# 48 unused columns instead of 16 between two groups of weight buffers in an encoder kernel

## The chip, the core and the metric

The kernel runs on one core of one Trainium2 chip, as one launch. The metric is the device time of that launch in microseconds (us); less is better. Before the change, three runs took 2910.47, 2912.47 and 2912.86 us: the median is 2912.47 us.

## What is computed

The reference is a two-layer bidirectional encoder on 256 tokens of width 2048, in float32. Nearly all of its arithmetic is in products of the 256 tokens with weight matrices:

```python
for i in range(DEPTH):                          # 2 layers
    h = rmsnorm(x, g_mix[i])
    z = h @ w_in[i]                             # q, k, v, two latents, rope key, two gates
    ...                                         # two kinds of attention: y_diff, y_mla
    merged = jax.nn.sigmoid(ga) * y_diff + jax.nn.sigmoid(gb) * y_mla
    x = x + merged @ w_out[i]
    gu = rmsnorm(x, g_ffn[i]) @ w_gate_up[i]    # 2048 -> 2 x 5632
    gate, up = jnp.split(gu, 2, axis=-1)
    x = x + (jax.nn.silu(gate) * up) @ w_down[i]
    e = p[i] @ w_ple_in[i]
    x = x + jax.nn.sigmoid(rmsnorm(x, g_ple[i]) @ w_ple_gate[i]) * e
return rmsnorm(x, g_final)
```

## The kernel before, in words

**A product in three parts.** Tokens lie along the columns, features along the 128 partitions. Each float32 number is cut in two numbers of the type fp32r: its leading bits ("hi") and the remainder ("lo"). A product of weights W and activations u is then W_hi·u_hi + W_hi·u_lo + W_lo·u_hi. An activation tile `ua[j]` or `ub[j]` (the operands) holds 256 columns of u_hi and behind them 256 columns of u_lo for one block of 128 features, so 512 columns or 2048 bytes in each partition.

For one block of 128 × 128 weights, `emit` issues two matmuls. The first (line 211) has 128 columns of `whi` as stationary operand and streams all 512 columns of the tile past them; the second (line 212) has 128 columns of `wlo` and streams the first 256 columns, u_hi. I call the two a pair. The profile shows each matmul as a weight load (PEld, LDWEIGHTS) and the matmul proper (PE, MATMUL). `product` runs 16 pairs into one PSUM bank for an output block of 128 features (8 to 16 for the other widths). Here are the lines:

```python
PE.matmul(acc, hi[:, s], u, start=start, stop=False)          # line 211: weights hi, 512 columns
PE.matmul(acc[:, T:], lo[:, s], u[:, :T], start=False, stop=stop)  # line 212: weights lo, 256 columns
```

**The weights' way.** `piece` fetches 1024 columns of float32 weights by one DMA from SyncE's queue into one of four buffers `w32`; ScalarE copies them to fp32r, which is `whi` (line 181, three buffers); VectorE subtracts, which gives `wlo` (line 74 through a helper, three buffers). One such piece serves 8 pairs.

**The values' product** (`values`, lines 392 to 394) is the other way round: slices of `ua` are stationary, and 512 columns of `whi` (lines 392 and 393) or `wlo` (line 394) stream past them. Attention's scores are line 341, its transposes 359, its outputs 563 and 620.

**What sets the order.** A scheduler at build time puts each engine's instructions in a fixed order, and the engines meet through semaphores. The stages follow the reference: values, latents, queries and keys between attention heads; the two gates (`wga`, `wgb`); the branch products (`w_bd`, `w_bm`); `w_out`; the feed-forward products; `w_pg`.

**Where the buffers lie.** Buffers are laid out one behind the other in each partition, in the order in which they are first asked for. Start addresses, modulo 256 bytes, before the change:

| buffers | bytes each | address modulo 256 |
|---|---|---|
| `ua`, `ub` (all 32) | 2048 | 128 |
| `xT`, `kr`, `fb`, `fc`, `fa5` to `fa7`, cosines and sines | 1024 and more | 128 |
| `ident`, `ones`, `fa0` to `fa4` | 512, 2048 | 32 |
| `w32` (4), `wlo` (3) | 4096 | 128 |
| `step` | 64 | 128 |
| `whi` (3) | 4096 | 192 |
| `E`, `join`, `a`, `sq`, `sh`, `E1`, `wt`, `sig`, `vals` | 1024 and more | 192 |
| `row`, `ssq`, `dg` | 1024 | 64 |

A slice of 128 columns is 512 bytes, so every slice of a buffer has that buffer's place modulo 256. Nothing reads `step`: it is set to zero once, by GpSimd, and keeps 16 columns (64 bytes) between `wlo` and what follows. It is made in `piece`, between `lo` and `hi`:

```python
if not step:
    step.append(wts.tile([P, STEP], F32, tag="step", name="step", bufs=1))
    nc.gpsimd.memset(step[0], 0.0)
hi = wts.tile([P, PT * P], F32R, tag="whi", name="whi", bufs=3)
```

Of the kernel before, what the change touches and what calls it, by code (L numbers as in the profile page):

```python
# [37 lines left out]
W_BUFS = 4  # L38
WARM = 8
PAD = 96  # L40
STEP = 16
NO_SYNC = mybir.DependencyInfo(mybir.DependencyClass.NoSync, mybir.DependencyReason.DATA)

TWO_PI = 2.0 * math.pi
# [8 lines left out]
def encoder(ctx, tc, x, p, positions, cols, lams, wq, wk, wv, wcq, wckv, wkr, wga, wgb,  # L53
# [114 lines left out]
    def piece(src, n):  # L168
# [3 lines left out]
# [3 lines that stand above are left out]
# [614 lines left out]
```

## Time and profile before

| what | value |
|---|---|
| median of three runs | 2912.47 us |
| the profiled execution's own time | 2910.11 us |
| its span, from the first instruction to the last | 2908.3 us |
| mean granted TensorE clock | 0.998 |
| TensorE busy with matmuls | 2890.7 us |
| VectorE, ScalarE busy | 2062.3 us, 1524.6 us |
| HBM read | 527.43 MB |

The profile comes from one execution. A row of a group names the line, the engine, the operation, what is written from what, the number of instructions, then the busy time, the mean duration of one in ns, and the idle time of the engine ahead of them. Matmuls are pipelined: the recorded duration of one reaches from its start to its modelled end and overlaps the next one's, so what one matmul costs is read from start to start.

### The profile page before, as it was taken

To read this page: it belongs to the slowest core of one execution; us is meant where nothing else is said; L and a number is where in the kernel's file an instruction comes from. 1 tells how busy PE (TensorE), PEld (TensorE's weight loads), DVE (VectorE), ACT (ScalarE), POOL (GpSimd) and SP (SyncE) were. 2 spreads that over 40 slices of the span, in tenths; PEclk is the share of its full clock that TensorE was granted. 3 is DMA by queue.
4 is the path that set the end of the run, shared out by engine and by line. 5 is a ranking of instruction groups with operands and counts; after the bars stand their busy time and mean duration, and the time that the engine had idled before them with its cause. 6 is when DMAs were issued, how large, how long until landed. Compare 5 with 4: busy or idle time off the path is not lost.

```text
span 2908.3 us, 43980 instructions
## 1 busy us (share of the span) xinstructions
PE 2890.7 (99%) x16750; PEld 2539.6 (87%) x16750; DVE 2062.3 (71%) x3529; ACT 1524.6 (52%) x2529; POOL 1.7 (0%) x9
## 2 busy tenths in 40 slices
PE   9999999999999999999999999999999999999998
PEld 7888888888888888888888888888888888888887
DVE  7897658776666666667859976687666666666676
ACT  6676545554444444454646755555444444444554
POOL 0000000000000000000000000000000000000000
PEclk9999999999999999999999999999999999999999
DMA  7554466555665566566565445666556655655664
GB/s 236 165 163 147 159 195 197 190 186 188 184 193 189 183 189 192 189 188 188 189 188 168 151 153 167 195 195 189 186 188 184 193 188 180 197 188 189 189 186 141
DMA packets 156019, 532.40 MB, mean 183 GB/s; under 512 B 16928, under 2 KB 23840, under 8 KB 155808
## 3 DMA queue, kind: packets, MB, share of 16 engines
q1 hardware_dynamic: 155376, 529.01, 57.9%
q8 instruction: 131, 2.15, 0.3%
q14 instruction: 80, 0.66, 0.1%
q10 hardware_dynamic: 432, 0.59, 0.1%
HBM read 527.43 MB, written 2.10 MB: 182 GB/s over the span
## 4 chain that ended last, share of the span: by engine, by line
PE 99%; DVE 1%; ACT 0%; DMA 0%; SPq 0%; issue 0%; DVEq 0%
PE mm L211 61%; PE mm L212 31%; PE S L341 1%; PE mmv L394 1%; PE mmv L392 1%; PE mmv L393 1%; PE at L359 0%; PE at L563 0%; PE at L620 0%; DMA w<-in_wv 0%; PE at L280 0%; DVE xT L74 0%; PE at L271 0%; DVE wlo L74 0%; ACT whi L181 0%; DVE a L74 0%
## 5 line engine op out<-in xcount | busy, mean ns | idle before, releaser
L181 ACT ACTIVATE whi<-w 128x1024 fp32r<-128x1024 f32 (+2 forms) x1029 | 1068.5, 1039 | 1311.4 <-issue 749.3
L74 DVE TENSOR_TENSOR wlo<-w,whi 128x1024 fp32r<-128x1024 f32 (+2 forms) x1029 | 1228.6, 1194 | 740.2 <-ACT whi L181 730.4
L211 PE MATMUL mm<-ub,whi 128*128 128x512 f32 x3952 | 1381.5, 394 | 0.0
L211 PE MATMUL mm<-ua,whi 128*128 128x512 f32 x3744 | 1307.8, 394 | 0.0
L212 PE MATMUL mm<-ub,wlo 128*128 128x256 f32 x3952 | 1107.7, 280 | 0.0
L212 PE MATMUL mm<-ua,wlo 128*128 128x256 f32 x3744 | 1048.5, 280 | 0.0
L211 PEld LDWEIGHTS mm<-ub,whi 128*128 128x128 f32 x3952 | 742.1, 188 | 164.5
L211 PEld LDWEIGHTS mm<-ua,whi 128*128 128x128 f32 x3744 | 702.5, 188 | 151.5
L212 PEld LDWEIGHTS mm<-ub,wlo 128*128 128x128 f32 x3952 | 749.0, 190 | 0.8
L212 PEld LDWEIGHTS mm<-ua,wlo 128*128 128x128 f32 x3744 | 708.2, 189 | 2.2 <-DVE wlo L74 0.4
L74 DVE TENSOR_TENSOR a<-mm,join 128x256 f32<-128x256 f32 x421 | 174.8, 416 | 0.3 <-ACT join L236 0.2
L236 ACT ACTIVATE join<-mm 128x256 f32<-128x256 f32 x453 | 165.9, 367 | 5.4 <-PE mm L212 5.0
L74 DVE TENSOR_TENSOR xT<-xT,mm 128x256 f32<-128x256 f32 x256 | 106.6, 419 | 48.4 <-PE mm L212 44.5
L74 DVE TENSOR_TENSOR a<-a,row 128x256 f32<-128x256 f32 x207 | 87.2, 424 | 6.6 <-ACT row L284 0.8
L74 DVE TENSOR_TENSOR a<-a 128x256 f32<-128x256 f32 x120 | 51.0, 425 | 4.0
L392 PE MATMUL mmv<-whi,ua 128*128 128x512 f32 x128 | 51.0, 399 | 2.0 <-ACT whi L181 2.0
L74 DVE TENSOR_TENSOR ua<-a,ua 128x256 fp32r<-128x256 f32 x120 | 50.1, 417 | 1.0 <-ACT ua L244 1.0
L393 PE MATMUL mmv<-whi,ua 128*128 128x512 f32 x128 | 50.5, 395 | 0.0
L244 ACT ACTIVATE ua<-a 128x256 fp32r<-128x256 f32 x120 | 48.2, 402 | 2.7 <-DVE a L74 2.6
L350 ACT ACTIVATE E<-S,nm 128x256 f32<-128x256 f32 x96 | 44.2, 470 | 5.1 <-DVE nm L80 5.0
L394 PE MATMUL mmv<-wlo,ua 128*128 128x512 f32 x128 | 46.8, 397 | 0.1
L74 DVE TENSOR_TENSOR ssq<-ssq,sq 128x256 f32<-128x256 f32 x97 | 40.5, 417 | 0.5 <-ACT sq L263 0.5
(154 smaller groups left out, 1158.9 us busy)
## 6 DMA issues: line engine op xcount, KB each, us to landing
w<-in_w_gate SPq DMA_DIRECT2D x176, 512.0 KB, 4.6
w<-in_w_up SPq DMA_DIRECT2D x176, 512.0 KB, 4.5
w<-in_w_down SPq DMA_DIRECT2D x128, 512.0 KB, 3.7
w<-in_wga SPq DMA_DIRECT2D x64, 512.0 KB, 3.8
w<-in_wgb SPq DMA_DIRECT2D x64, 512.0 KB, 4.5
w<-in_w_out SPq DMA_DIRECT2D x64, 512.0 KB, 4.2
w<-in_w_pg SPq DMA_DIRECT2D x64, 512.0 KB, 4.4
w<-in_w_down SPq DMA_DIRECT2D x64, 384.0 KB, 3.6
```

What stands on the lines that cost most here:

```text
L74: return V.tensor_tensor(out=o, in0=a, in1=b, op=op)
L181: last_split[:] = A.activation(hi[:, :m], w[:, :m], AF.Copy), tt(lo[:, :m], w[:, :m], hi[:, :m].bitcast(F32), ALU.subtract)
L211: PE.matmul(acc, hi[:, s], u, start=start, stop=False)
L212: PE.matmul(acc[:, T:], lo[:, s], u[:, :T], start=False, stop=stop)
L236: A.activation(t, acc[:, T:], AF.Copy)
L244: return A.activation(hi, src, AF.Copy), tt(lo, src, hi.bitcast(F32), ALU.subtract)
L341: PE.matmul(S[:, b, :], q[:, b * P : (b + 1) * P], k, start=j == 0, stop=j == len(pairs) - 1)
L350: last_exp[0] = A.activation(E[:, b, :], S[:, b, :], AF.Exp, bias=nm[:, b : b + 1], scale=scale, accum_out=sm[:, b : b + 1])
L392: PE.matmul(banks[b], xh, hi[:, s], start=a + j == 0, stop=False)
L393: PE.matmul(banks[b], xl, hi[:, s], start=False, stop=False)
L394: last_mm[:] = [PE.matmul(banks[b], xh, lo[:, s], start=False, stop=a + j == n - 1)]
```

## The change

One constant is changed, and with it the size of `step`:

```diff
@@ -38,7 +38,7 @@
 WARM = 8
 PAD = 96
-STEP = 16
+STEP = 48
```

`step` has 192 bytes instead of 64, so everything behind it lies 128 bytes further on: `whi`, and all buffers of the pools for temporary tiles and statistics. `ua`, `ub`, `w32`, `wlo` and all tiles ahead of them stay where they are. Modulo 256, `whi` goes from 192 to 64: from 64 bytes behind the operands' place to 64 bytes ahead of it. `E`, `join`, `a`, `vals`, `wt` and their like go from 192 to 64 too, and `row`, `ssq`, `dg` from 64 to 192. The instructions of every engine and their order are the same, but for the size of one memset on GpSimd.

## The prediction

> **What bounds the kernel now.** I read the page first: busy shares, granted clock, and the chain of work that ended last.
>
> ```profile
> PE 2890.7 (99%) x16750; PEld 2539.6 (87%) x16750; DVE 2062.3 (71%) x3529; ACT 1524.6 (52%) x2529; POOL 1.7 (0%) x9
> ...
> PEclk9999999999999999999999999999999999999999
> ...
> PE 99%; DVE 1%; ACT 0%; DMA 0%; SPq 0%; issue 0%; DVEq 0%
> ```
>
> TensorE is busy in 99% of the span, at full clock in every slice, and the chain runs through it for 99%. Whether it waits for anybody is answered by the waits of PE and PEld; these are the longest rows of each:
>
> ```profile
> PE at L280 <- DVE dg L80: 2.7, 1, 2.7
> PE at L271 <- ACT ssq L260: 2.0, 1, 2.0
> ...
> PEld mmv L392 <- ACT whi L181: 2.8, 2, 1.5
> ```
>
> Waits of 2.7 us in 2908.3 are nothing: the time is the matmuls' own pace, so only a change of pace can show. The page's groups say which matmuls:
>
> ```profile
> L74 DVE TENSOR_TENSOR wlo<-w,whi 128x1024 fp32r<-128x1024 f32 (+2 forms) x1029 | 1228.6, 1194 | 740.2 <-ACT whi L181 730.4
> L211 PE MATMUL mm<-ub,whi 128*128 128x512 f32 x3952 | 1381.5, 394 | 0.0
> L211 PE MATMUL mm<-ua,whi 128*128 128x512 f32 x3744 | 1307.8, 394 | 0.0
> L212 PE MATMUL mm<-ub,wlo 128*128 128x256 f32 x3952 | 1107.7, 280 | 0.0
> L212 PE MATMUL mm<-ua,wlo 128*128 128x256 f32 x3744 | 1048.5, 280 | 0.0
> ```
>
> There are 3952 + 3744 = 7696 pairs. So 1 ns on each pair is 7.7 us, or 0.26% of the time. Durations overlap, so the pace comes from the starts. The timeline in a long feed-forward stretch:
>
> ```profile
> 1101.93 0.39 PE L211 MATMUL mm<-ub,whi 128*128 128x512 f32 x1
> 1101.93 0.19 PEld L212 LDWEIGHTS mm<-ub,wlo 128*128 128x128 f32 x1
> 1102.16 0.28 PE L212 MATMUL mm<-ub,wlo 128*128 128x256 f32 x1
> 1102.16 0.19 PEld L211 LDWEIGHTS mm<-ub,whi 128*128 128x128 f32 x1
> 1102.28 0.40 PE L211 MATMUL mm<-ub,whi 128*128 128x512 f32 x1
> ```
>
> Two things are to be seen. From one line 211 to the next it is 0.35 us: 0.23 for 512 columns and 0.12 for 256. And each weight load starts together with the matmul ahead of its own. So while line 212 streams u_hi (place 128 modulo 256), the next `whi` is loaded (192 before, 64 after); while line 211 streams, `wlo` is loaded (128, as before). The change touches the first of these two overlaps and leaves the second.
>
> Is 0.35 us the pace everywhere? Busy time and count of line 211 in stretches of the span (us, then PE busy with its count; length over count is the pace):
>
> ```profile
> 346.00:529.00 183.00, 182.27 (x537) 100.62 (x536) 1.00 0.62 197
> 529.00:627.00 98.00, 97.41 (x280) 52.34 (x280) 1.00 0.59 188
> 627.00:1450.00 823.00, 822.07 (x2350) 440.94 (x2349) 1.00 0.61 188
> ...
> 1500.00:1550.00 50.00, 48.93 (x144) 26.85 (x143) 1.00 0.58 183
> ...
> 1786.00:1970.00 184.00, 183.27 (x540) 101.17 (x539) 1.00 0.61 197
> 2068.00:2885.00 817.00, 816.07 (x2332) 437.70 (x2332) 1.00 0.60 187
> ```
>
> It is not. 98/280, 823/2350 and 817/2332 are 350 ns a pair; 183/537 and 184/540 are 341, and 50/144 is 347 with its edges in it. From the starts inside these quick stretches:
>
> ```profile
> 399.68 0.39 PE L211 MATMUL mm<-ua,whi 128*128 128x512 f32 x1
> ...
> 400.02 0.39 PE L211 MATMUL mm<-ua,whi 128*128 128x512 f32 x1
> ...
> 401.04 0.39 PE L211 MATMUL mm<-ua,whi 128*128 128x512 f32 x1
> ```
>
> 1.36 us for four pairs: 340 ns. The tiles, the buffers and all their places are the same as in the slow stretches, and other engines' work is much alike. So there are two paces, 340 and 350, that the pair can settle in, and once in one it stays for hundreds of pairs. At equal addresses the phase between load and stream, set by what ran just ahead, decides which. The addresses can only decide which paces exist and how easily each is entered.
>
> **The change, part by part.** The larger memset runs on GpSimd, which is busy for 1.7 us in all, and nobody waits for `step`: nothing. ScalarE writes `whi`, VectorE reads it, and both write and read the shifted temporaries. Should an access cost them something there, the group of `wlo` above bounds what is harmless: one split takes 1.19 us, one piece lasts 8 pairs or 2.8 us, and VectorE idles for 740.2 us ahead of these instructions. Up to some 0.7 us more for each of the 1029 splits is hidden under the matmuls; without that cover each would cost its own excess. I take 0.
>
> On TensorE, line 212's overlap counts. I look for the nearest rows with a load at the stream's place less 64: the values' product. There `whi` (192) streams while a slice of `ua` or `ub` (128) is loaded, in lines 392 and 393: 128 − 192 = −64. In line 394 `wlo` streams (128): difference 0. Each line by itself (duration min/median/max in ns), with scores that have difference 0 behind them:
>
> ```profile
> L392 PE MATMUL mmv<-whi,ua x128: 387/394/793, 4.6 to 1496.0; 128*128 128x512 f32 x128
> L392 PE MATMUL mmv<-whi,ub x16: 391/396/401, 231.1 to 1680.6; 128*128 128x512 f32 x16
> L393 PE MATMUL mmv<-whi,ua x128: 388/393/612, 5.2 to 1496.3; 128*128 128x512 f32 x128
> L393 PE MATMUL mmv<-whi,ub x16: 391/396/398, 231.3 to 1680.8; 128*128 128x512 f32 x16
> L394 PE MATMUL mmv<-wlo,ua x128: 388/393/578, 6.1 to 1496.5; 128*128 128x512 f32 x128
> L394 PE MATMUL mmv<-wlo,ub x16: 389/398/401, 231.5 to 1681.0; 128*128 128x512 f32 x16
> ...
> L341 PE MATMUL S<-kr,fc x48: 279/283/284, 285.4 to 1768.5; 128*128 128x256 f32 x48
> ```
>
> In the same products, difference −64 has medians of 393.5 (the two lines with `ua`) and 396 (with `ub`), difference 0 has 393 and 398. Weighted by 128 and 16, −64 is (128 × 0.5 − 16 × 2)/144 = 0.2 ns dearer than 0. Line 211, also at 0, has 394 as its mean. So −64 looks no different from the places already in use, and all of these rows spread by 5 to 9 ns between minimum and median, as two paces 10 ns apart for two matmuls would make them. The step from −64 against 0 to −64 against +64 is a choice: line 212 at +64 has a mean of 280, and the scores at 0 a median of 283, which lets +64 be up to 3 ns better than 0. I take 0.2 ns on 7696 pairs, 1.5 us, as the likeliest, and keep both ends: below, all pairs at 340; above, 3 ns on each load and the quick stretches lost.
>
> The rest of TensorE: the 2 × 144 matmuls of lines 392 and 393 go from −64 to +64, and the transposes (line 359) read `E` at another distance from `ident`. Even ±3 ns on 288 + 128 of them is 1.2 us. The scores read only tiles that stay. Lines 563 and 620 have both operands among the shifted ones. I take 0.
>
> The sum: 2910.1 us of the profiled execution + 1.5 = 2911.6; the median of the runs shown lies 2.4 us above that execution, so 2914 us.
>
> A rule that bears on this stands in the Trainium skill, "TensorE: Matmul & The Clock Gate", section "Part 2: What happens when you issue a matmul": TensorE has two independent read ports into SBUF, and loading the next weights takes nothing from the running matmul. The same page's "Back-to-back issue gap" has N/2.4 + 2.5 ns, which I work out, as an estimate, to 215.8 + 109.2 = 325 ns for a pair. The trace disagrees with the second, 340 and 350 ns measured, and two paces at one clock are hard to have if streams and loads never meet. By the first rule the sum would be 2912.5 exactly.
>
> **The rivals.**
>
> *Nothing at all (D).* If the two paces come from the order of issue alone and places in SBUF don't matter, every stretch stays as it is: 2912.5 us. For it: equal addresses give both paces. Against it: something has to make 340 into 350, and the median of 283 for scores against 280 for line 212 goes with the place. The Trainium skill's rule on the two ports, above, would give the same.
>
> *The quick pace spreads (B).* At 340 ns in all stretches, the 7696 − 537 − 144 − 540 = 6475 pairs at 350 save 10 ns each: 65 us, to 2848 us. For it: 340 is stable over 500 pairs and differs from 350 only in how it was entered; line 393 reaches the low 388 ns at −64 too. Against: the values' medians at −64 sit with the slow pace. Half of the stretches would give 2880.
>
> *A heavier pace (C).* The load of `whi` at −64 falls on the stream at a worse moment. It shows in line 212, which would go from 280 to 283 or more, and it decides against the change as soon as the quick stretches go: their 537 + 144 + 540 = 1221 pairs at 350 cost 12 us, 2925 us; 3 ns more on every line 212 is another 23, 2948 us; if line 211 is pulled along by 3 ns as well, 2971. For it: 396 in the rows with `ub`, 283 in the scores. Against: 16 instructions each, between other work.
>
> **How the numbers follow.** The forecast (A), two paces much as now with some shift in the quick share, has 0.34: 2906 to 2926 by itself, about half of it within 0.2%. D has 0.10, B 0.30, C 0.26. A difference under 0.2%, 5.8 us, can't be told from none. Faster: 0.30 from B and 0.06 from A. Same: 0.16 from A and 0.10 from D. Slower: 0.26 from C and 0.12 from A. The range goes from B's end, 2848, to C's, 2971; beyond lie a pace under 340, and loads that cost over 3 ns on both matmuls, together under 0.2.
>
> **What would show it.** Right: starts of line 211 still 350 ns apart in the long stretches (about 2350 in 627 to 1450 us) and 340 in 346 to 529 us; mean of line 212 within 1 ns of 280. B: counts near 2420 in 823 us. C: line 212 at 283 or more, no stretch at 340. Wrong in the whole reasoning: TensorE waiting for `whi` or `wlo`, or a pace that differs by stage with no relation to these two.

## The result, and the profile after

The kernel takes 2868.07 us (median of 6 runs, 2865.90 to 2868.81) against 2911.7 us before: a ratio of 0.985, interval 0.9837 to 0.9863. It is faster by 1.5%, a small change but clear of the noise. The profiled execution took 2867.58 us with a span of 2865.8 us, 42.5 us less than that of before. My forecast was no change, 2914 us; the time lies in the stated range, near the side of the rival "the quick pace spreads".

The page after, busy shares and the two matmul groups of the pairs:

```profile
PE 2845.8 (99%) x16750; PEld 2507.7 (88%) x16750; DVE 2063.3 (72%) x3529; ACT 1524.2 (53%) x2529; POOL 1.7 (0%) x9
...
PEclk9999999999999999999999999999999999999999
...
L211 PE MATMUL mm<-ub,whi 128*128 128x512 f32 x3952 | 1360.8, 392 | 0.0
L211 PE MATMUL mm<-ua,whi 128*128 128x512 f32 x3744 | 1283.4, 390 | 0.0
L212 PE MATMUL mm<-ub,wlo 128*128 128x256 f32 x3952 | 1096.8, 278 | 0.0
L212 PE MATMUL mm<-ua,wlo 128*128 128x256 f32 x3744 | 1036.3, 277 | 0.0
```

TensorE is still the bound, at the same clock. Its busy time fell by 44.9 us and the span by 42.5, so the gain is all in the matmuls' pace. Both matmuls of a pair last a little less (line 211 from 394 to 391 ns on average, line 212 from 280 to 277.5), but durations overlap; what a pair costs is read from the starts. Over some 7500 pairs that follow each other directly, a pair takes 342.1 ns on average against 348.1 before. Line 211 (from its start to that of line 212) went from 231.2 to 227.9, line 212 from 116.9 to 114.2. VectorE and ScalarE are as busy as before.

Where? Line 211's count in stretches of the span after (the columns are the stretch, its length, PE busy with the count, PEld busy with its count, clock, DMA share, GB/s):

```profile
346.00:517.00 171.00, 171.00 (x504) 94.38 (x504) 1.00 0.61 195
528.00:604.00 76.00, 76.00 (x224) 41.91 (x224) 1.00 0.60 195
623.00:768.00 145.00, 144.85 (x414) 77.83 (x414) 1.00 0.59 186
840.00:990.00 150.00, 150.00 (x442) 82.80 (x442) 1.00 0.59 192
1100.00:1250.00 150.00, 150.00 (x442) 82.77 (x441) 1.00 0.60 194
1356.00:1427.00 71.00, 71.00 (x203) 38.02 (x203) 1.00 0.60 189
```

150/442 and 171/504 are 339 ns, 145/414 and 71/203 are 350. (A count takes in the matmuls that reach over the edges of its stretch, so length over count reads up to about 1 ns low: by the starts, 1100 to 1250 us is at 350.0 ns before and 340.0 after.) So there are again two paces, 340 and 350, and the quick one now holds nearly everywhere: 5920 of the 7500 pairs take at most 343 ns, against 1546 before. These 4374 pairs at 10 ns each are 44 us. Slow are, apart from a few short pieces, two stretches in each layer, those behind the two norms of the feed-forward and gate parts. The start of the gate part's shows how the pace is lost there, at four small matmuls of the norm (line 271):

```profile
1345.41 0.39 PE L211 MATMUL mm<-ub,whi 128*128 128x512 f32 x1
...
1345.75 0.39 PE L211 MATMUL mm<-ub,whi 128*128 128x512 f32 x1
...
1346.10 0.50 PE L271 MATMUL at<-ones,ssq 128*128 128x1 f32 x4
...
1346.89 0.40 PE L211 MATMUL mm<-ub,whi 128*128 128x512 f32 x1
...
1347.24 0.40 PE L211 MATMUL mm<-ub,whi 128*128 128x512 f32 x1
...
1347.59 0.40 PE L211 MATMUL mm<-ub,whi 128*128 128x512 f32 x1
```

Ahead of them it is 340 ns from start to start, behind them 350. The slow pace isn't quite that of before, either: there line 211's durations alternate, 0.39 and 0.40 us, and the pairs take 348 and 352 ns (or 349 and 351) in turn; here each pair takes 350.

### The profile page after: what moved, and what is told of

The parts are those of the page before. It is cut to its first block, busy times and chain, and to the rows that moved or that the text cites. A ratio compares the mean times of both kernels' runs of the same rounds, so it can differ in the third digit from the quotient of the medians.

```text
span 2865.8 us, 43980 instructions
## 1 busy us (share of the span) xinstructions
PE 2845.8 (99%) x16750; PEld 2507.7 (88%) x16750; DVE 2063.3 (72%) x3529; ACT 1524.2 (53%) x2529; POOL 1.7 (0%) x9
## 4 chain that ended last, share of the span: by engine, by line
PE 98%; DVE 1%; ACT 0%; DMA 0%; issue 0%; SPq 0%; DVEq 0%
PE mm L211 61%; PE mm L212 31%; PE S L341 1%; PE mmv L394 1%; PE mmv L393 1%; PE mmv L392 1%; PE at L359 0%; PE at L563 0%; PE at L620 0%; DMA w<-in_wv 0%; DVE wlo L74 0%; DVE a L74 0%; PE at L280 0%; DVE xT L74 0%; ACT E L350 0%
## 5 line engine op out<-in xcount | busy, mean ns | idle before, releaser
L211 PE MATMUL mm<-ub,whi 128*128 128x512 f32 x3952 | 1360.8, 392 | 0.0
L211 PE MATMUL mm<-ua,whi 128*128 128x512 f32 x3744 | 1283.4, 390 | 0.0
L212 PE MATMUL mm<-ua,wlo 128*128 128x256 f32 x3744 | 1036.3, 277 | 0.0
```

## The experiments

Three theories stood at the start. **Place**: the place of `whi` against the operands decides. **Temporaries**: the tiles that moved along, which stand in the matmuls between stretches, set the phase at which a stretch is entered. **Lots**: any shift draws the entries anew, with no rule.

### Which of the moved buffers does it

`whi` moved alone, or everything else moved alone; a second unused tile behind `whi` does it, and the order of instructions stays that of before.

```diff
 # whi moved alone
-STEP = 16
+STEP = 48
 # both runs
         hi = wts.tile([P, PT * P], F32R, tag="whi", name="whi", bufs=3)
+        if len(step) == 1:
+            step.append(wts.tile([P, 32], F32, tag="behind", name="behind", bufs=1))
+            nc.gpsimd.memset(step[1], 0.0)
```

`whi` alone. Expected:

> whi at the operands' place less 64 as after the change, all temporary tiles back at their places of before (32 unused columns behind whi). If the place of whi against the operands decides (theory 1): 2868 us, within 6 us, and 340 ns a pair in the same long stretches as after. If the moved temporaries, which are stationary or streamed in the matmuls between the stretches, set the phase at which a stretch is entered (theory 2): 2912 us. If any shift draws the entries anew, with no rule (theory 3): any value between 2850 and 2925, as likely near one as near the other.

Measured: 2867.08 us (ratio 0.9851, 0.9835 to 0.9867). The stretches of the matmul with `whi`, same columns:

```profile
346.00:515.00 169.00, 169.00 (x498) 93.30 (x497) 1.00 0.61 195
621.00:759.00 138.00, 137.80 (x394) 73.89 (x393) 1.00 0.59 186
840.00:988.00 148.00, 148.00 (x437) 81.76 (x436) 1.00 0.61 192
1100.00:1249.00 149.00, 149.00 (x439) 82.24 (x439) 1.00 0.61 194
```

The whole gain is there, with the same slow stretch behind the norm (138/394 is 350) between the same quick ones. What the place of `whi` is counted from isn't shown by this: `ua` and `ub` were never moved, and no run moved `whi` by a full 256 bytes. "Against the operands" and "modulo 256" are my way of naming a place.

The temporaries alone. Expected:

> The counterpart: whi at the operands' place plus 64 as before the change, the temporaries 128 bytes further on as after it. Theory 1 (place of whi): 2912 us and 350 ns in the long stretches. Theory 2 (temporaries): 2868 us. Theory 3 (no rule): anywhere between 2850 and 2925 us.

Measured: 2922.0 us (ratio 1.004, 1.0025 to 1.0054), so it costs 11 us.

```profile
350.00:520.00 170.00, 170.00 (x487) 91.24 (x486) 1.00 0.59 190
...
1100.00:1250.00 150.00, 150.00 (x430) 80.54 (x429) 1.00 0.59 189
```

The stretch at 350 to 520 us, at 340 ns before the change (183/537 in 346 to 529), is now at 170/487 = 349. In the second layer it is the same (175/501 = 349 in 1800 to 1975 us, against 184/540 before), and these two stretches, some 1060 pairs at 10 ns, are the 11 us. So the theory of the temporaries isn't empty, as they decide how the long stretch behind attention is entered when `whi` lies at +64; but they give none of the gain. With `whi` at −64 their place makes no difference: 2867.08 and 2868.07 us. Lots fall with the first of the two runs, which repeated after's stretches one by one.

### Other places

`STEP` was set to 0, 32, 40 and 56; then `wlo` was moved as well. The diffs:

```diff
-STEP = 48
+STEP = 32          # and 40, and 56; for 0, step isn't made at all
 # both weight parts at the operands' place less 64: step ahead of lo
+        if not step:
+            step.append(wts.tile([P, STEP], F32, tag="step", name="step", bufs=1))
+            nc.gpsimd.memset(step[0], 0.0)
         lo = wts.tile([P, PT * P], F32R, tag="wlo", name="wlo", bufs=3)
-        if not step:
-            step.append(wts.tile([P, STEP], F32, tag="step", name="step", bufs=1))
-            nc.gpsimd.memset(step[0], 0.0)
 # wlo at +64, whi at 0: 16 columns ahead of lo, 48 between lo and hi
```

> No unused columns: whi, wlo and the operands all at the same place modulo 256. Theory 1: another share of the quick pace, which the scores with a difference of 0 (120 ns for 256 columns) suggest is small: 2915 to 2930 us, two paces of 340 and 350 or a heavier one near 352. Theory 3: anywhere between 2850 and 2930 us.

> 32 unused columns: whi at the operands' place plus 128 modulo 256, half way round. Theory 1: a time of its own that the places on both sides don't give; if what counts is how far the load lies behind the stream, between 2868 and 2912 us. Theory 2 and 3: anywhere between 2850 and 2930 us.

> whi at the operands' place less 96. If the quick pace at -64 needs that place exactly: other paces than 340 and 350, as with 0 and 32 columns, 2915 to 2940 us. If it is enough that the load lies well behind the stream: 2850 to 2880 us.

> whi at the operands' place less 32. If the place has to be exact: 2915 to 2940 us. If it is enough to lie behind the stream: 2850 to 2880 us.

> The 48 unused columns ahead of wlo instead of behind it: both weight parts at the operands' place less 64. If a place of -64 helps each load by itself, the 512-column matmul gains as well: 2850 us or less. If the pace hangs on the two loads' places together, it may be any of the paces seen: 2850 to 2940 us.

> wlo at the operands' place plus 64 and whi at the operands' place: the two parts lie to each other as after the change (whi 64 less than wlo), and both 64 further from the operands. If the distance between the two parts decides: 2868 us. If their places against the operands decide: another time, 2880 to 2940 us.

Measured, one run each (medians for the second and third row), with line 211's count in the 150 us from 1100 to 1250 us of each profile, all inside the long feed-forward stretch. In every row the temporaries move along with `whi`:

| place of `wlo`, `whi` against the operands | us | count in 150 us | ns a pair |
|---|---|---|---|
| 0, 0 | 2920.38 | 434 | 346 |
| 0, +64 (before) | 2911.7 | 430 | 349 |
| 0, −64 (after) | 2868.07 | 442 | 339 |
| 0, +128 | 2939.85 | 427 | 351 |
| 0, −96 | 2921.15 | 430 | 349 |
| 0, −32 | 2888.25 | 437 | 343 |
| −64, −64 | 2938.06 | 426 | 352 |
| +64, 0 | 2901.12 | 433 | 346 |

The rows of 1100 to 1250 us, of before, of −32, and of both parts at −64:

```profile
1100.00:1250.00 150.00, 150.00 (x430) 80.54 (x429) 1.00 0.59 188
```

```profile
1100.00:1250.00 150.00, 150.00 (x437) 81.58 (x436) 1.00 0.60 192
```

```profile
1100.00:1250.00 150.00, 150.00 (x426) 79.70 (x425) 1.00 0.60 190
```

The count is that of this stretch alone: at 0, 0 the stretch of 350 to 500 us has 424 pairs, 354 ns, so the whole is slower than 346 suggests. The times also hold what the temporaries do, 11 us in the one case where they were moved alone; the count in the long stretch didn't change there (430). Still, nearly every place has a pace of its own, and the times don't follow the distance. At −96 it is 2921 us, as expected if the quick pace needs −64 exactly; but −32 gives 343 ns and 2888 us, neither of the two paces and neither of the two times expected. +128, 2940 us, has a time of its own, outside what the other theories allowed. A place of −64 is no good in itself, since with both parts there the time is among the worst. (Against the kernel after, `wlo` alone has moved in that run: `whi` and the temporaries keep their addresses.) Nor does the distance between the two parts decide: +64 and 0 lie to each other as 0 and −64 do, and take 33 us more. So the place of one part alone doesn't give the pace: it takes the places of both, together.

### The order of matmuls

At −64 two paces remain. Is a stretch slow for the work that it does, or for the way in which it was entered? The order of two matmuls in single products was changed: hi0 lo0 hi1 lo1 to hi0 hi1 lo0 lo1, the same work. (The lines that choose the products are left out here.)

```diff
-                PE.matmul(acc[:, T:], lo[:, s], u[:, :T], start=False, stop=stop)
+                late.append((lo[:, s], u, stop)); [PE.matmul(acc[:, T:], w, v[:, :T], start=False, stop=e) for w, v, e in ([] if j == 0 and first and len(us) > 1 and kicks and kicks.pop() else [late.pop(0) for _ in list(late)])]
```

First once behind each norm.

> The kernel after, with two matmuls changed in their order at four places: in the first product behind each of the four norms of the feed-forward and gate parts, hi0 lo0 hi1 lo1 becomes hi0 hi1 lo0 lo1. Entry theory (the phase at which a stretch begins decides its pace): the four stretches that run at 350 ns behind those norms (about 397 and 208 pairs in the first layer, 397 and 192 in the second, with their neighbours some 1240 pairs) go to 340 and save 10 ns each: 2868 - 12 = 2856 us. Rival (these stretches are slow for what they do: their weights, their DMA traffic or the work of the other engines): nothing changes, 2868 us.

Measured: 2868.77 us (ratio to the kernel before 0.9855, 0.9838 to 0.9871), no change from the kernel after, and the stretch 623 to 761 us still has 394 pairs, 350 ns. The profile shows why this decides little: in the feed-forward part the changed product ran at 617 us, ahead of the norm's last matmuls at 623 us, so it met the quick pace and left it quick. In the gate part it fell into the slow stretch and left that slow.

Then at the start of every product, with `whi` at −64 and at +64. The build-time scheduler gives the program another order for this, the same in both.

> The kernel after, with the same change of order at the start of every product, so that each of some 500 products begins anew from the same disturbance. Entry theory: with whi at -64 nearly every product settles at 340 ns within a few pairs; the disturbance itself costs some 30 ns each, 500 x 30 = 15 us, so about 2865 us. Rival (chance at every entry): a mixture of products at 340 and at 350.

> The kernel before with the same order as the previous one: whi at +64, all else equal. Entry theory: the same disturbance leads to 350 ns here in nearly every product, 2920 to 2930 us. Rival (chance at every entry): the same mixture as with whi at -64, and the two times within 10 us of each other.

Measured: 2873.37 and 2923.79 us, one run each. Line 211 in 1100 to 1250 us, at −64 and at +64:

```profile
1100.00:1250.00 150.00, 148.20 (x440) 80.32 (x439) 1.00 0.60 192
```

```profile
1100.00:1250.00 150.00, 148.11 (x430) 78.70 (x429) 1.00 0.60 190
```

Equal orders, a disturbance in every product, and 50 us between them: at −64 the pairs return to the quick pace in nearly every product, at +64 in hardly any. That is no mixture. (The time at −64 is 8 us above the 2865 expected.)

Then six kinds of changed order, one product each, in the slow feed-forward stretch of both layers. The matmuls of a piece are issued through a list, which a table reorders:

```diff
-STEP = 48
+STEP = 48; KINDS = {(0, 2): [(0, 2, 1, 3)], (0, 4): [(0, 1, 3, 2)], ...}   # 2j: hi of block j, 2j+1: lo
-                a = pre.pop(0) if pre else joined(product(w_gate[L, f], ub))
+                kinds.extend(KINDS.get((L, f), ())); a = pre.pop(0) if pre else joined(product(w_gate[L, f], ub))
```

> The kernel after, with the order of single products changed in the stretch that runs at 350 ns behind the first feed-forward norm of each layer. First layer, products of w_gate: number 2 hi0 hi1 lo0 lo1; 4 hi0 lo0 lo1 hi1; 6 three hi then three lo; 8 hi0 hi1 lo1 lo0; 10 eight hi then eight lo; 12 hi0 lo0 lo1 hi1 hi2 lo2. Second layer: the same kinds in another sequence. Entry theory: at least one kind takes the stretch to 340 ns, and from there to the stretch's end it stays there, at the same work: up to 14 us less than 2868. If these stretches are slow for what they do: no kind changes the pace for more than its own pairs, 2868 us.

> whi at +64, the same order of all instructions as the run in which single products of the slow feed-forward stretches got another order at -64; there the pace came to 340 ns behind several of the kinds and stayed through most of the following ones. If 340 is merely entered more often at -64 by chance of the order: here too it is entered at one kind or another and stays through some, and the time falls by 3 us or more against 2911. If at +64 an order out of step loses 340 and doesn't win it back: at most one or two of the twelve kinds are followed by 340, the next one ends it, and the time is 2909 to 2913 us.

Measured: 2862.55 us at −64 and 2911.6 us at +64. At −64, the stretches between changed products:

```profile
623.00:629.00 6.00, 5.80 (x17) 3.00 (x17) 1.00 0.63 200
630.00:738.00 108.00, 106.81 (x318) 59.26 (x318) 1.00 0.61 194
740.00:769.00 29.00, 29.00 (x84) 15.60 (x83) 1.00 0.59 175
```

At 629 us the first kind (hi0 hi1 lo0 lo1) turns 350 into 340 (108/318), which then lasts through four more changes; only the last kind (hi0 lo0 lo1 hi1 hi2 lo2, at 738 us) loses it. In the second layer that kind loses it too, and the one behind it brings it back. So these stretches aren't slow for their work, though one pass of this saves 5.5 us of the 14 that I had allowed: the first layer's stretch is lost again at 738 us, and the gate part stays as it is.

At +64, same order, the first two kinds lead to no quick pace; the third (three hi, then three lo, at 680 us) does. The timeline of the fourth change (hi0 hi1 lo1 lo0) shows the loss 22 us later, and the row of line 211 behind it the pace that stays, 73/209 = 349:

```profile
701.51 0.39 PE L211 MATMUL mm<-ub,whi 128*128 128x512 f32 x1
701.73 0.28 PE L212 MATMUL mm<-ub,wlo 128*128 128x256 f32 x1
701.85 0.39 PE L211 MATMUL mm<-ub,whi 128*128 128x512 f32 x1
...
702.19 0.62 PE L211 MATMUL mm<-ub,whi 128*128 128x512 f32 x2
702.65 0.40 PE L212 MATMUL mm<-ub,wlo 128*128 128x256 f32 x2
702.88 0.40 PE L211 MATMUL mm<-ub,whi 128*128 128x512 f32 x1
...
703.23 0.39 PE L211 MATMUL mm<-ub,whi 128*128 128x512 f32 x1
703.58 0.40 PE L211 MATMUL mm<-ub,whi 128*128 128x512 f32 x1
```

```profile
703.00:776.00 73.00, 72.02 (x209) 39.01 (x209) 1.00 0.59 184
```

701.51 to 701.85 is 340 ns; then come two line 211 in a row at 702.19, and 703.23 to 703.58 is 350. In the second layer it went alike: 340 behind the same kind, at 2143 us, and lost at the next one (hi0 lo0 lo1 hi1), at 2165 us. So the quick pace can be entered at +64 and doesn't last there, which is the second of the two cases expected, and the time is that of before.

Last, the consequence: at −64, hi0 hi1 lo0 lo1 in three products close behind each norm, so that one miss is followed by another try.

> The kernel after, with hi0 hi1 lo0 lo1 at the start of three products close behind each of the four norms, so that one miss is followed by another try. Entry theory: the stretches that ran at 350 ns behind the norms (about 1240 pairs) change to 340 within a few microseconds of the norm, 2868 - 12 + 1 = 2856 to 2858 us, faster than both kernels. If the pace behind the norms of the gate part can't be changed in this way (one try left it at 350): only the two feed-forward stretches change, some 840 pairs, 2860 us. If order has no lasting effect: 2868 us.

Measured: 2855.72 us (5 runs, 2855.34 to 2857.55; ratio to the kernel before 0.9809, 0.9796 to 0.9823), faster than both kernels. The feed-forward stretch, the gate stretch, and the second layer's feed-forward stretch:

```profile
629.00:757.00 128.00, 127.87 (x377) 70.48 (x377) 1.00 0.61 191
1359.00:1421.00 62.00, 61.93 (x183) 34.12 (x183) 1.00 0.63 195
...
2065.00:2171.00 106.00, 106.00 (x313) 58.49 (x312) 1.00 0.61 191
```

All are at 339 to 340 ns. The same change of order in the same kernel, at −64 and already quick, leaves it quick (two line 211 in a row at 638.66, and 340 ns again from 640.05 on):

```profile
637.98 0.39 PE L211 MATMUL mm<-ub,whi 128*128 128x512 f32 x1
638.32 0.39 PE L211 MATMUL mm<-ub,whi 128*128 128x512 f32 x1
...
638.66 0.62 PE L211 MATMUL mm<-ub,whi 128*128 128x512 f32 x2
639.12 0.39 PE L212 MATMUL mm<-ub,wlo 128*128 128x256 f32 x2
639.35 0.40 PE L211 MATMUL mm<-ub,whi 128*128 128x512 f32 x1
...
640.05 0.39 PE L211 MATMUL mm<-ub,whi 128*128 128x512 f32 x1
640.39 0.39 PE L211 MATMUL mm<-ub,whi 128*128 128x512 f32 x1
```

## Why the prediction was wrong

**Right**: TensorE's pace is the bound and nobody makes it wait; the larger memset, ScalarE and VectorE cost nothing (VectorE is busy for 2063.3 us against 2062.3). There are two paces at equal addresses, 340 and 350, and what interrupts the pairs decides between them. B's 65 us for all slow pairs was about the right size: 42.5 came, and the version with a changed order behind the norms has 12 more. By the starts it is nearer 60, since 1546 pairs were quick before and not the 1221 of three stretches.

**Wrong, the step that failed**: the price of line 212's overlap, "0.2 ns" dearer for each pair, from the nearest rows. Measured, a pair became 6 ns cheaper on average. The step took the difference of places of one load and one stream as the thing that has a price, and the values' product as its witness; and it said that the change leaves the other overlap, `wlo` loaded while line 211 streams. But of the 6 ns, 3.3 came from line 211, where neither the stream nor the load has moved, and 2.7 from line 212. The cost belongs to the repeating sequence and not to one overlap. The witness shows the same after the change:

```profile
L393 PE MATMUL mmv<-whi,ua x128: 387/398/401, 5.2 to 1475.0; 128*128 128x512 f32 x128
...
L394 PE MATMUL mmv<-wlo,ua x128: 388/397/580, 5.9 to 1475.3; 128*128 128x512 f32 x128
```

Line 394, whose own load and stream kept their places (difference 0), went from a median of 393 to 397. Its mean duration stayed at 397, but from start to start, in the 69 rounds of the three lines with nothing between, it went from 232 to 235 ns. And with `wlo` and `whi` both at −64, line 212 streams and loads at the same places as after the change, yet takes 120 ns from start to start in 1100 to 1250 us, against 113 after: a price that hangs on that distance alone would have left it at 113.

**The choice between A and B** failed with it. I kept the share of the quick pace near its value before, since I had no row on what a place does to that share, and counted the values' medians at −64 against B. Between +64 and −64 the place changes just that share: at −64 the pairs come back to 340 after most changes of order and most breaks between stages, at +64 they mostly go to 350. It is no rule without exception, as the norms of the feed-forward and gate parts lead to 350 at −64 too. The trace of before held a hint that I didn't use: the quick stretches ended at a boundary between stages, at 529 us, and the pairs behind it stayed slow for hundreds of us. The question to ask was how stable each pace is against such an interruption, and medians of another sequence couldn't answer it.

**The other rivals.** D, nothing at all, falls: `whi` alone moves the time by 44 us. The rule of the Trainium skill ("TensorE: Matmul & The Clock Gate", section "Part 2: What happens when you issue a matmul") that the next weights' load takes nothing from the running matmul would give 2912.5 us; these runs disagree with that time, with 2867 to 2940 us from places alone, though none of them shows what a load takes. C, a heavier pace at −64, didn't come; such paces do exist at other places (351 ns at +128, 352 with both parts at −64).

**Open**: why −64 lets the pairs return to 340, and whether it is the distance to the operands or the place by itself that does it. No run here shows which accesses meet, none moved `ua` and `ub`, and none was made that measures loads and streams by themselves at each place.

## What to carry to other kernels

Where TensorE is busy throughout and still slower than its best stretch, compare its pace from start to start in several stretches: paces that differ at equal work and clock are time to be had. The places of the weight buffers in SBUF, and the order of matmuls after an interruption, both changed the pace here; try places in a sweep, with all operands of the loop together, as single distances predicted nothing here. Rows from another sequence of matmuls don't price such a move.

## What the runs showed of the hardware that was not expected

- A repeating pair of matmuls (512 and 256 columns of fp32r, each beside a weight load) settles at 340 or 350 ns at the same addresses and a clock of 1.00, and stays there, for up to 1400 pairs, until other matmuls or another order interrupt it. This is so at −64 and +64; other places gave other paces, 343 to 352 ns.
- Moving one weight buffer by 128 bytes, nothing else changed, takes this kernel from 2911 to 2867 us. With the temporaries moving along, six places of that buffer within 256 bytes give 2868 to 2940 us, 2.5%.
- Two pairs in another order (hi hi lo lo, at −64) can turn a stretch of hundreds of pairs from 350 to 340 ns; another such order (hi hi lo lo with the two lo exchanged, at +64) turned one from 340 to 350.
